# Second accumulator banks for the up products, bias columns inside evictions, and a gathered modulation in a diffusion step

## The chip, the cores and the metric

One core of a Trainium2 chip runs one step of a small hybrid diffusion network. The metric is the device time of one execution in microseconds.

## The reference

The input is 128 prompt and 512 latent tokens of 1024 features. Two layers each compute half a SwiGLU, a token mixer, and another half a SwiGLU. Before every sub-layer the tokens are normalised, scaled and shifted; scale, shift and gate (nine vectors of 1024 per layer, for two conditions) come from a linear map of the condition:

```python
def ada_modulation(cond, w, b):
    m = jax.nn.silu(cond) @ w + b
    return m.reshape(cond.shape[0], 1, 9, D_MODEL)

def half_ffn(x, g, mod, j, w13, w2):
    gt, up = jnp.split(ada_norm(x, g, mod, j) @ w13, 2, axis=-1)
    return x + 0.5 * mod[:, :, 3 * j + 2] * ((jax.nn.silu(gt) * up) @ w2)
```

Layer 0 mixes by windowed attention and a long convolution side by side, layer 1 by a gated DeltaNet in both directions. All is float32.

## The kernel before, in words

Everything is feature-major: a tile is 128 features by 640 tokens, and a product of 640 tokens is made in two halves of 320 in two banks of PSUM. Each float32 operand is split into a rounded part (hi) and a rest (lo), and a product is hi x hi, hi x lo and lo x hi. The weights are split on the chip: line 452 (ScalarE) makes hi and line 453 (VectorE) makes lo. The split weights lie in a ring of six slots.

A feed-forward part (`ffn_s`, four of them) handles the 22 feature tiles of the hidden layer in chunks of 7, 7 and 8. For each tile the gate and the up projection are one 2 x 2 block product, done with seven products of half the depth in place of eight, in the order q0, q3, q4, q1, q5, q2, q6. Each q is 12 matmuls of 322 columns (320 tokens and two columns that carry the shift's product, the bias, for the two conditions). q0 and q1 go to bank a, q3 and q2 to c, q4 to d, q5 to e, and q6 to d again; these are banks 4 to 7 for every tile but the second:

```python
a, c, d, e = [self.ps[:, b, :] for b in ((2, 3, 0, 1) if ci == 0 and m == 1 else range(4, 8))]
dst = (a, a, c, c, d, e, d)[q]
```

ScalarE copies q0 and q3 out of PSUM (line 783). VectorE evicts q4 (789), q1 (798), q5 (793), q2 (802) and q6 (807) over 320 columns, and the bias columns by a small operation of their own after each (791, 800, 794, 808). GpSimd adds and scales (795, 796, and 809 after 807). Line 803 scales on VectorE, and lines 804 and 805 are Silu on ScalarE. `finish` multiplies (756, 757, of which 756 reads what 809 writes) and splits (758, 759). It is called when q3 of the next tile has been written. The sums of weights that the seven products need are four GpSimd operations a tile (447); they read the loaded weights and the sums' buffers are read by lines 452 and 453.

After a chunk's up products its down products follow: eight feature tiles t, each of 42 or 48 matmuls (line 482) into a pair of banks that `wide` hands out in turn, 0 and 1 or 2 and 3. `x_add` (737) adds each to the residual in three operations: prompt, latent tokens of the first half, second half.

The first part also makes most of layer 0's modulation vectors. `ada_small` is a generator that `ffn_s` advances by one step before each q. A block is 128 features: two loads of 256 KB (577, on SP's queue, which also issues the weights' loads at 463), eight small matmuls (582), an eviction (584), a transpose (587), and on VectorE a reduction (551) and a bias (552). There are 48 blocks of three steps, with banks 0 and 1 in turn.

Each engine works its instructions off in a fixed order, which a scheduler makes at build time from the program's order and a priority; line 453's split, for one, is moved ahead by 30 and line 783 by 150.

## Time and profile before

| what | value |
|---|---|
| runs | 3068.59, 3074.09, 3074.75 us, median 3074.09 |
| profiled execution, its span | 3072.3 us, 1.8 below the median |
| TensorE, VectorE busy | 94%, 74% |
| ScalarE, GpSimd busy | 42%, 38% |

The profiled execution is one execution; the page gives no time of its own for it beside the span. The page has the busy shares first, then the groups by line with the idle time before them and what ended it. A time view shows instructions in order with their start in microseconds from the span's start. PE is TensorE, PEld its weight loads, DVE VectorE, ACT ScalarE, POOL GpSimd, SPq the queue of loads that SyncE issues.

### The profile page before, as it was taken

Reading aid. Unit: us, or ns where it says so; the run is one execution under the profiler, and the core shown is the slowest. Engines: PE = TensorE matmul, PEld = TensorE weight load, DVE = VectorE, ACT = ScalarE, POOL = GpSimd, SP = SyncE. Lnnn points to the kernel's source line nnn. Section 1 sums busy time; section 2 is a strip of 40 time slices with the busy share of each in tenths; the row PEclk is TensorE's granted clock in tenths of the full one; section 3 lists DMA queues with packets and bytes.
Section 4 is the critical chain, followed back from the end, with each engine's and each line's share of the span. In section 5 each row is a group of like instructions: output and inputs, shape, how many; then the busy total and the mean of one; then the engine's idle time right before and its main releaser. Section 6 shows DMA issues by size and latency. Waiting matters only on the chain. (4 is left out here: it accounts for less than half of the span.)

```text
span 3072.3 us, 54018 instructions
## 1 busy us (share of the span) xinstructions
PE 2903.3 (94%) x20612; PEld 2683.4 (87%) x20612; DVE 2263.2 (74%) x5235; ACT 1303.0 (42%) x2678; POOL 1158.2 (38%) x955
## 2 busy tenths in 40 slices
PE   5999999999989899999999999999998999999999
PEld 3999999977766899999899999978878888899999
DVE  6858586687865785858785858679898967858584
ACT  4424243466522342424342424445555544424241
POOL 3525253101222563535563535332222224626361
PEclk7999999999989999999999999999999999999999
DMA  5434353334375122222122222322211112222222
GB/s 202 141 107 150 105 158 121 122 105 125 100 274 206 63 72 84 85 74 89 50 74 85 84 75 84 131 91 70 72 59 34 34 37 94 68 77 74 84 70 83
DMA packets 109439, 300.80 MB, mean 98 GB/s; under 512 B 11803, under 2 KB 31963, under 8 KB 104444
## 3 DMA queue, kind: packets, MB, share of 16 engines
q1 hardware_dynamic: 109180, 297.35, 29.1%
q8 instruction: 162, 2.65, 0.4%
q14 instruction: 97, 0.79, 0.1%
HBM read 277.38 MB, written 19.93 MB: 97 GB/s over the span
## 5 line engine op out<-in xcount | busy, mean ns | idle before, releaser
L453 DVE TENSOR_TENSOR wh<-base,wh 128x512 fp32r<-128x512 f32 (+2 forms) x746 | 745.7, 1002 | 122.0 <-PE psum L482 62.6
L452 ACT ACTIVATE wh<-base 128x512 fp32r<-128x512 f32 (+2 forms) x779 | 533.7, 706 | 669.1 <-PE psum L482 400.8
L447 POOL TENSOR_TENSOR base<-base 128x512 f32<-128x512 f32 x352 | 518.1, 1476 | 683.9 <-DMA base<-w 364.1
L482 PE MATMUL psum<-G,wh 128*128 128x320 f32 x4992 | 742.5, 310 | 8.5 <-DVE base L737 8.0
L482 PEld LDWEIGHTS psum<-G,wh 128*128 128x128 f32 x4992 | 737.0, 188 | 13.4 <-issue 7.5
L778 PE MATMUL psum<-H,wh 128*128 128x322 f32 x4224 | 700.7, 317 | 22.6 <-ACT H L659 11.8
L778 PEld LDWEIGHTS psum<-H,wh 128*128 128x128 f32 x4224 | 648.0, 192 | 41.6 <-ACT H L659 13.8
L778 PE MATMUL psum<-HX,wh 128*128 128x322 f32 x3168 | 527.5, 316 | 27.5 <-DVE base L808 21.7
L778 PEld LDWEIGHTS psum<-HX,wh 128*128 128x128 f32 x3168 | 482.0, 191 | 44.0 <-issue 31.8
L482 PE MATMUL psum<-H,wh 128*128 128x322 f32 (+1 forms) x2448 | 476.7, 330 | 3.6 <-DVE base L722 2.1
L482 PEld LDWEIGHTS psum<-H,wh 128*128 128x128 f32 x2448 | 375.3, 193 | 25.8 <-issue 17.7
L737 DVE SCALAR_TENSOR_TENSOR base<-psum,base 128x128 f32<-128x128 f32 x336 | 127.1, 433 | 211.6 <-PE psum L482 211.5
L453 POOL TENSOR_TENSOR wh<-base,wh 128x1024 fp32r<-128x1024 f32 x33 | 82.2, 2491 | 239.5 <-ACT wh L452 234.8
L795 POOL TENSOR_TENSOR base<-base 128x320 f32<-128x320 f32 x88 | 113.1, 1285 | 143.4 <-DVE base L794 133.6
L805 ACT ACTIVATE base<-base 128x512 f32<-128x512 f32 x88 | 63.6, 723 | 204.0 <-DVE base L803 204.0
L758 ACT ACTIVATE G<-base 128x640 fp32r<-128x640 f32 x88 | 65.1, 740 | 167.0 <-DVE base L757 156.8
L756 DVE SCALAR_TENSOR_TENSOR base<-base 128x128 f32<-128x128 f32 x88 | 32.9, 374 | 120.0 <-POOL base L809 120.0
L694 POOL TENSOR_TENSOR base<-base 128x640 f32<-128x640 f32 x30 | 77.7, 2589 | 110.9 <-ACT base L692 94.7
L796 POOL TENSOR_TENSOR base<-base 128x320 f32<-128x320 f32 x88 | 87.8, 998 | 6.9
L809 POOL TENSOR_TENSOR base<-base 128x320 f32<-128x320 f32 x88 | 76.2, 866 | 28.9 <-DVE base L808 28.9
L803 DVE TENSOR_TENSOR base<-base 128x320 f32<-128x320 f32 x88 | 85.1, 967 | 0.4
L759 DVE TENSOR_TENSOR G<-base,G 128x640 fp32r<-128x640 f32 x88 | 71.8, 816 | 15.0 <-ACT G L758 14.9
(702 smaller groups left out, 3764.6 us busy)
## 6 DMA issues: line engine op xcount, KB each, us to landing
base<-w SPq DMA_DIRECT2D x208, 512.0 KB, 3.2
base<-ada_w SPq DMA_DIRECT2D x128, 256.0 KB, 3.7
base<-w SPq DMA_DIRECT2D x64, 448.0 KB, 3.3
base<-dn_in SPq DMA_DIRECT2D x33, 512.0 KB, 3.3
base<-ada_w SPq DMA_DIRECT2D x14, 1024.0 KB, 5.0
G<-ada_w SPq DMA_DIRECT2D x48, 256.0 KB, 3.5
HX<-ada_w SPq DMA_DIRECT2D x10, 1024.0 KB, 4.9
base<-mx_in SPq DMA_DIRECT2D x18, 512.0 KB, 3.3
```

Of the source, the lines that this page charges most:

```text
L447: nc.gpsimd.tensor_tensor(out=out, in0=x, in1=y, op=op)
L452: nc.scalar.activation(out=hi, in_=src, func=AF.Copy)
L453: (self.lo_eng if q is None else nc.vector).tensor_tensor(out=lo, in0=src, in1=hif, op=ALU.subtract)
L482: nc.tensor.matmul(ps[:, h, :n], lhsT=w[:, k, :], rhs=m[k][:, HALF * h:HALF * h + n], start=start and k == 0 and w is hi and m is mh, stop ...
L694: nc.gpsimd.tensor_tensor(out=self.acc.f, in0=self.acc.f, in1=sq, op=ALU.add)
L737: nc.vector.scalar_tensor_tensor(out=xt[:, xo:xo + n], in0=ps[:, h, o:o + n], scalar=gate[:, t, c:c + 1], in1=xt[:, xo:xo + n], op0=ALU.mu ...
L759: TT(out=gl[m], in0=tu, in1=gf[m], op=ALU.subtract)
L778: nc.tensor.matmul(dst[:, :HB], lhsT=w[:, i, :], rhs=v[:, i, :], start=not more and i == 0 and n == 0, stop=i == 3 and n == 2, skip_group_ ...
L795: nc.gpsimd.tensor_tensor(out=p5, in0=u2[:, 0, :HALF], in1=p5, op=ALU.add)
L796: nc.gpsimd.tensor_tensor(out=u2[:, 1, :HALF], in0=p5, in1=fac[:, 1], op=ALU.mult)
L803: TT(out=g2[:, 1, :HALF], in0=g2[:, 1, :HALF], in1=fac[:, 1], op=ALU.mult)
L809: nc.gpsimd.tensor_tensor(out=u2[:, 0, :HALF], in0=u2[:, 0, :HALF], in1=fac[:, 0], op=ALU.mult)
```

## The change

- The up products: bank pairs (4, 5) and (2, 3) alternate from tile to tile for a and c; d is 6, e is 7, and q6 has bank 0 to itself.
- The bias columns are evicted with their 320 columns, by one operation of 322; the buffers are longer by the two columns, and the scale is 1.0 in them. Silu and the product in `finish` take the bias from there. Silu is three operations in place of two, since the two bias columns lie in the middle.
- The two halves of a wide product lie side by side over the border of two banks (192 to 512 of the first, 0 to 320 of the second), so `x_add` takes two operations.
- `ada_four` replaces `ada_small` in the first part: four blocks gather in one bank, then one eviction, four transposes, one reduction and one bias for the four. Its next loads are issued after a block's matmuls. 48 blocks take two steps each, three where the four are full. It has bank 1, and the wide products of this part have banks 2 to 5.

```diff
         self.modA = [arena.alloc(48) for _ in range(2)]
-        self.rstd, self.rms = [arena.alloc(NT) for _ in range(2)]
+        self.rstd, self.rms = [arena.alloc(2 * HB) for _ in range(2)]
+        nc.gpsimd.memset(self.rms.f[:, HALF:HB], 1.0)
...
         self.mm_i += 1
-        return self.ps[:, b:b + 2, :]
+        return self.ps[:, b:b + 2, :].rearrange("p b n -> p (b n)")[:, 512 - HALF:]
...
                         n = HALF + extra * h
-                        nc.tensor.matmul(ps[:, h, :n], lhsT=w[:, k, :], rhs=m[k][:, HALF * h:HALF * h + n],
+                        nc.tensor.matmul(ps[:, HALF * h:HALF * h + n], lhsT=w[:, k, :], rhs=m[k][:, HALF * h:HALF * h + n],
...
 
-    def ada_bufs(self, A, low=False):
-        return [A.alloc(n, low) for n in (512, 512, 128)]
+    def ada_four(self, items, rg, bufs):
+        nc = self.nc
+        e = bufs[2].f
+        sc = self.scond.f.rearrange("p (k m) -> p k m", m=32)
+        todo = [(l, 2 * j + q, b) for l, j in items for q in range(2) for b in range(4)]
+        def load(i):
+            l, n, b = todo[i]
+            for h in range(2):
+                nc.sync.dma_start(out=bufs[h].f, in_=self.io["ada_w"][l, n, h][:, 512 * b:512 * b + 512])
+        load(0)
+        yield 0.0
+        for i, (l, n, b) in enumerate(todo):
+            p = rg.bank()
+            for h in range(2):
+                for g in range(4):
+                    nc.tensor.matmul(p[32 * g:32 * g + 32, 128 * b:128 * b + 128], lhsT=sc[:, 4 * h + g, :], rhs=bufs[h].f[:, 128 * g:128 * g + 128],
+                                     start=h == 0, stop=h == 1, tile_position=(0, 32 * g))
+            if i + 1 < len(todo):
+                load(i + 1)
+            yield 450.0
+            if b == 3:
+                nc.scalar.activation(out=e, in_=p, func=AF.Copy)
+                yield 0.0
+                self.ada_turn(l, n, e, rg)
+                yield 440.0
+            else:
+                yield 0.0
+        for b in bufs:
+            b.free()
+    def ada_bufs(self, A, low=False, n=128):
+        return [A.alloc(n, low) for n in (512, 512, n)]
...
         if self.sums is None:
-            self.sums, self.fac = [self.A.arenas[0].alloc(n, True) for n in (2048, NT)]
+            self.sums, self.fac = [self.A.arenas[0].alloc(n, True) for n in (2048, 2 * HB)]
+            self.nc.gpsimd.memset(self.fac.f[:, HALF:HB], 1.0)
...
         nc = self.nc
-        for (h, o, n, xo, c) in ((0, 0, NP, 0, 0), (0, NP, HALF - NP, NP, 1), (1, 0, HALF, HALF, 1)):
-            nc.vector.scalar_tensor_tensor(out=xt[:, xo:xo + n], in0=ps[:, h, o:o + n], scalar=gate[:, t, c:c + 1],
-                                           in1=xt[:, xo:xo + n], op0=ALU.mult, op1=ALU.add)
+        for c, v in enumerate((slice(0, NP), slice(NP, NT))):
+            nc.vector.scalar_tensor_tensor(out=xt[:, v], in0=ps[:, v], scalar=gate[:, t, c:c + 1], in1=xt[:, v], op0=ALU.mult, op1=ALU.add)
...
         part = [A.alloc(n, True) for n in (HB, HALF)]
-        tmp = [[A.alloc(NT, True) for _ in range(2)] for _ in range(2)]
+        tmp = [[A.alloc(2 * HB, True) for _ in range(2)] for _ in range(2)]
...
 
-        def finish(m, tg, tu, bu):
-            nc.vector.scalar_tensor_tensor(out=tu[:, :NP], in0=tu[:, :NP], scalar=bu[:, 0:1], in1=tg[:, :NP], op0=ALU.add, op1=ALU.mult)
-            nc.vector.scalar_tensor_tensor(out=tu[:, NP:], in0=tu[:, NP:], scalar=bu[:, 1:2], in1=tg[:, NP:], op0=ALU.add, op1=ALU.mult)
-            nc.scalar.activation(out=gh[m], in_=tu, func=AF.Copy)
-            TT(out=gl[m], in0=tu, in1=gf[m], op=ALU.subtract)
+        def finish(m, tg, tu):
+            for k, v in enumerate((slice(0, NP), slice(NP, NX))):
+                nc.vector.scalar_tensor_tensor(out=tg[:, v], in0=tu[:, v], scalar=tu[:, HALF + k:HALF + k + 1], in1=tg[:, v],
+                                               op0=ALU.add, op1=ALU.mult)
+            v = halves(tg)[:, :, :HALF]
+            nc.scalar.activation(out=halves(gh[m]), in_=v, func=AF.Copy)
+            TT(out=halves(gl[m]), in0=v, in1=halves(gf[m]), op=ALU.subtract)
...
                 p1, p5, tg, tu = [b.f for b in part + tmp[ti % 2]]
+                g2, u2 = halves(tg), halves(tu)
+                first = ci == 0 and m == 0
+                a, c = [self.ps[:, b, :] for b in ((4, 5), (2, 3))[ti % 2]]
+                d, e, d2 = [self.ps[:, b, :] for b in ((1, 7, 0) if ti == 1 and not ready else (6, 7, 0))]
                 ti += 1
-                g2, u2 = halves(tg), halves(tu)
-                a, c, d, e = [self.ps[:, b, :] for b in ((2, 3, 0, 1) if ci == 0 and m == 1 else range(4, 8))]
-                first = ci == 0 and m == 0
...
                     mh, ml, _ = P[q]
-                    dst = (a, a, c, c, d, e, d)[q]
+                    dst = (a, a, c, c, d, e, d2)[q]
...
                             fac = halves(self.norm.f)
-                        TT(out=g2[:, 1, :HALF], in0=d[:, :HALF], in1=p1[:, :HALF], op=ALU.add)
-                        bu = self.bias2()
-                        TT(out=bu, in0=d[:, HALF:HB], in1=p1[:, HALF:], op=ALU.add)
+                        TT(out=g2[:, 1], in0=d[:, :HB], in1=p1, op=ALU.add)
                     elif q == 5:
-                        TT(out=u2[:, 0, :HALF], in0=e[:, :HALF], in1=g2[:, 1, :HALF], op=ALU.add)
-                        TT(out=bu, in0=e[:, HALF:HB], in1=bu, op=ALU.add)
+                        TT(out=u2[:, 0], in0=e[:, :HB], in1=g2[:, 1], op=ALU.add)
                         nc.gpsimd.tensor_tensor(out=p5, in0=u2[:, 0, :HALF], in1=p5, op=ALU.add)
-                        nc.gpsimd.tensor_tensor(out=u2[:, 1, :HALF], in0=p5, in1=fac[:, 1], op=ALU.mult)
+                        nc.gpsimd.tensor_tensor(out=u2[:, 1, :HALF], in0=p5, in1=fac[:, 1, :HALF], op=ALU.mult)
                     if q == 1 and not first or q == 5 and first:
-                        TT(out=g2[:, 0, :HALF], in0=a[:, :HALF], in1=fac[:, 0], op=ALU.mult)
-                        bg = self.bias2()
-                        nc.vector.tensor_copy(out=bg, in_=a[:, HALF:HB])
+                        TT(out=g2[:, 0], in0=a[:, :HB], in1=fac[:, 0], op=ALU.mult)
...
                         TT(out=g2[:, 1, :HALF], in0=c[:, :HALF], in1=g2[:, 1, :HALF], op=ALU.add)
-                        TT(out=g2[:, 1, :HALF], in0=g2[:, 1, :HALF], in1=fac[:, 1], op=ALU.mult)
-                        nc.scalar.activation(out=tg[:, :NP], in_=tg[:, :NP], func=AF.Silu, bias=bg[:, 0:1])
-                        nc.scalar.activation(out=tg[:, NP:], in_=tg[:, NP:], func=AF.Silu, bias=bg[:, 1:2])
+                        TT(out=g2[:, 1, :HALF], in0=g2[:, 1, :HALF], in1=fac[:, 1, :HALF], op=ALU.mult)
+                        for v, k in ((slice(0, NP), 0), (slice(NP, HALF), 1), (slice(HB, NX), 1)):
+                            nc.scalar.activation(out=tg[:, v], in_=tg[:, v], func=AF.Silu, bias=tg[:, HALF + k:HALF + k + 1])
                     if q == 6:
-                        TT(out=u2[:, 0, :HALF], in0=d[:, :HALF], in1=u2[:, 0, :HALF], op=ALU.add)
-                        TT(out=bu, in0=d[:, HALF:HB], in1=bu, op=ALU.add)
-                        nc.gpsimd.tensor_tensor(out=u2[:, 0, :HALF], in0=u2[:, 0, :HALF], in1=fac[:, 0], op=ALU.mult)
-                        tail = (m, tg, tu, bu)
+                        TT(out=u2[:, 0], in0=dst[:, :HB], in1=u2[:, 0], op=ALU.add)
+                        nc.gpsimd.tensor_tensor(out=u2[:, 0, :HALF], in0=u2[:, 0, :HALF], in1=fac[:, 0, :HALF], op=ALU.mult)
+                        tail = (m, tg, tu)
...
 
+        s.wides = [2, 4]
...
         g = s.ffn_s(0, 0, lambda t, xt, tn, sq: s.make_h(t, 0, 1, xt, tn, sq), True,
-                    s.ada_small([(0, j) for j in range(2, 8)], s.ring(0, 1), s.ada_bufs(arena, True)), ready)
+                    s.ada_four([(0, j) for j in range(2, 8)], s.ring(1), s.ada_bufs(arena, True, 512)), ready)
         run(g)
+        s.wides = [0, 2]
```

VectorE's order in the second part, from the end of one tile's evictions into the next tile. Before:

```order
L453 TENSOR_TENSOR wh<-base,wh 128x512
L803 TENSOR_TENSOR base<-base 128x320
L807 TENSOR_TENSOR base<-psum,base 128x320
L808 TENSOR_TENSOR base<-psum,base 128x2
L756 SCALAR_TENSOR_TENSOR base<-base 128x128
L453 TENSOR_TENSOR wh<-base,wh 128x512
L757 SCALAR_TENSOR_TENSOR base<-base 128x512
L453 TENSOR_TENSOR wh<-base,wh 128x512
```

Now (454 is 453 before, 835 is 803, 839 is 807, 791 is 756 and 757):

```order
L454 TENSOR_TENSOR wh<-base,wh 128x512
L835 TENSOR_TENSOR base<-base 128x320
L839 TENSOR_TENSOR base<-psum,base 128x322
L454 TENSOR_TENSOR wh<-base,wh 128x512
L791 SCALAR_TENSOR_TENSOR base<-base 128x128
L791 SCALAR_TENSOR_TENSOR base<-base 128x514
L454 TENSOR_TENSOR wh<-base,wh 128x512
```

A conversion of weights now stands between q6's eviction and the product in `finish`; the other conversions kept their places.

TensorE's order in the first part, up products with the blocks of modulation between them. Before:

```order
L582 MATMUL psum<-base 32x128 x8
L778 MATMUL psum<-H,wh 128x322 x12
L587 MATMUL psum<-base 128x128
L778 MATMUL psum<-HX,wh 128x322 x12
L778 MATMUL psum<-H,wh 128x322 x12
L582 MATMUL psum<-base 32x128 x8
```

Now (613 is 582 before, 815 is 778, 1153 is the transposes):

```order
L613 MATMUL psum<-base 32x128 x8
L815 MATMUL psum<-H,wh 128x322 x24
L1153 MATMUL psum<-base 128x128 x4
L815 MATMUL psum<-HX,wh 128x322 x12
L613 MATMUL psum<-base 32x128 x8
L815 MATMUL psum<-H,wh 128x322 x12
L815 MATMUL psum<-HX,wh 128x322 x12
L613 MATMUL psum<-base 32x128 x8
```

There were 36 up products between two blocks and a transpose with each; now there are 24, and 36 with four transposes after each fourth block. The transposes come 24 products after the fourth block and 12 before the next.

## Rows read from the trace of the kernel before

**Rows 1.** Page, costliest groups: line engine op, names, shapes xcount | busy, mean ns | idle before
```profile
L482 PE MATMUL psum<-G,wh 128*128 128x320 f32 x4992 | 742.5, 310 | 8.5 <-DVE base L737 8.0
```

**Rows 2.** Waits of TensorE, 1000 to 2000 us: us in total, times, longest
```profile
PE psum L778 <- DVE base L808: 12.6, 21, 0.8
```

**Rows 3.** Order of time, tile of part two: start us, us, instruction xcount [idle before]
```profile
1255.58 0.35 DVE L756 SCALAR_TENSOR_TENSOR base<-base 128x128 f32<-128x128 f32 x1 [2.14 <-POOL base L809]
...
1260.56 0.15 DVE L791 TENSOR_TENSOR base<-psum,base 128x2 f32<-128x2 f32 x1
1260.62 0.68 DVE L453 TENSOR_TENSOR wh<-base,wh 128x512 fp32r<-128x512 f32 x1
...
1262.40 2.99 POOL L447 TENSOR_TENSOR base<-base 128x512 f32<-128x512 f32 x2 [4.05 <-DVE wh L453]
...
1262.76 1.49 DVE L453 TENSOR_TENSOR wh<-base,wh 128x512 fp32r<-128x512 f32 x1
...
1267.59 1.29 POOL L447 TENSOR_TENSOR base<-base 128x512 f32<-128x512 f32 x1
1267.60 1.78 PEld L778 LDWEIGHTS psum<-HX,wh 128*128 128x128 f32 x12 [1.05 <-issue]
1267.63 2.02 PE L778 MATMUL psum<-HX,wh 128*128 128x322 f32 x12 [0.82 <-DVE base L808]
...
1268.84 0.75 POOL L809 TENSOR_TENSOR base<-base 128x320 f32<-128x320 f32 x1
...
1269.63 0.35 DVE L756 SCALAR_TENSOR_TENSOR base<-base 128x128 f32<-128x128 f32 x1 [2.14 <-POOL base L809]
```

**Rows 4.** Order of time, line 807: first and last of 24 long tiles
```profile
1140.17 0.48 DVE L807 TENSOR_TENSOR base<-psum,base 128x320 f32<-128x320 f32 x1
...
2988.86 0.48 DVE L807 TENSOR_TENSOR base<-psum,base 128x320 f32<-128x320 f32 x1
```

**Rows 5.** Order of time, part one: modulation blocks, their loads (SPq), transposes, reduction
```profile
240.57 0.14 PEld L587 LDWEIGHTS psum<-base 128*128 128x128 f32 x1
...
243.17 0.16 DVE L551 TENSOR_REDUCE base<-psum 128x2 f32<-128x8 f32 x1
...
244.49 0.64 PE L582 MATMUL psum<-base 128*32 128x128 f32 x16
...
245.30 0.33 SPq L463 DMA_DIRECT2D base<-w  x1
245.72 0.86 SPq L577 DMA_DIRECT2D base<-ada_w  x2
...
264.11 0.65 PE L582 MATMUL psum<-base 128*32 128x128 f32 x16
...
264.59 0.80 SPq L577 DMA_DIRECT2D base<-ada_w  x2
...
270.33 0.64 PE L582 MATMUL psum<-base 128*32 128x128 f32 x16
```

**Rows 6.** Line 577: landing of the second load at 265.0, first load at 245.7
```profile
DMA to landing us min/median/max: 3.4/3.4/3.4
...
DMA to landing us min/median/max: 4.2/4.2/4.2
```

**Rows 7.** Waits of TensorE's weight loads, 66 to 489 us
```profile
PEld psum L587 <- ACT base L584: 4.5, 8, 0.9
```

**Rows 8.** Order of time, part two, end of a chunk's up and down products
```profile
1303.20 5.91 PEld L482 LDWEIGHTS psum<-G,wh 128*128 128x128 f32 x40
...
1304.02 0.15 DVE L808 TENSOR_TENSOR base<-psum,base 128x2 f32<-128x2 f32 x1
...
1352.48 3.61 PEld L778 LDWEIGHTS psum<-H,wh 128*128 128x128 f32 x24
...
1353.81 1.13 DVE L737 SCALAR_TENSOR_TENSOR base<-psum,base 128x128 f32<-128x128 f32 x3
```

**Rows 9.** Page, costliest groups: the residual adds
```profile
L737 DVE SCALAR_TENSOR_TENSOR base<-psum,base 128x128 f32<-128x128 f32 x336 | 127.1, 433 | 211.6 <-PE psum L482 211.5
```

16 lines of the change are left out of this document (8 added, 8 removed).

## The prediction, before the result was known

> **What bounds the kernel now.** I read the page's busy shares first, then the groups by line, then TensorE's waits, and last the order of time around one tile. TensorE is busy nearly all the time, so the change can only win what TensorE loses in waits, and can lose whatever new waits it makes. The down products are almost free of waits: 4992 of them waited 8.5 us in all, 8.0 of it for the residual add at line 737 [rows 1]. The up products wait mostly for line 808, the last two bias columns of bank d: 12.6 us, 21 times, in the second and third feed-forward part together [rows 2].
>
> The steady tile shows what stands behind that wait [rows 3]. The reader is to see two loops there. One is TensorE's: q6's eviction runs late on VectorE, and the next product into its bank d waits for line 808 until 1267.63; its weight load had stood idle for 1.05 us. The other has no TensorE in it. VectorE stands idle for 2.14 us at line 756 until GpSimd's line 809 is done; 809 is the last of a row that GpSimd works through from 1262.40 without a gap (two sums of weights, 795, 796, one sum, 809) to 1269.59, 7.2 us. The row starts when VectorE's conversion before it is done, and from line 756 at 1255.58 VectorE needs 6.8 us to get there. 7.2 + 6.8 is the tile's period: 1255.58 to 1269.63, 14.05 us. TensorE alone would need 7 x 1.78 (the weight loads of 12 products [rows 3]) = 12.5 us. In the second to fourth part 24 tiles took 13.9 us or more, the first and last of them ending at line 807 in [rows 4], and nine 13.1 to 13.5. The first part differs: there the modulation's products are added to TensorE's, and one block of them follows the other every 6.22 us, from 264.11 to 270.33 [rows 5].
>
> **The change part by part**, against the profiled span of 3072.3 us, which lies 1.8 us below the median of the runs (3074.09; I add these 1.8 at the end).
>
> *Banks of the up products.* The waits for lines 802 and 808 go. But what is late next is the VectorE and GpSimd loop, and no bank is part of it. The reordered row shows what it gains: of the small operations, 791 and 800 lie in its VectorE half and cost 0.06 us each there (1260.56 to 1260.62 [rows 3]; the listed 0.15 overlaps its successor), so 0.13; and one conversion, 0.60 us, moves from behind the wait to ahead of it. That gives 14.05 - 0.73 = 13.3 us, if the moved conversion doesn't delay GpSimd. It may: beside GpSimd a conversion took 1.49 us in place of 0.68, and GpSimd's two sums took 2.99 us, where one alone takes 1.29 [rows 3]; so two contended conversions cost GpSimd 0.4 us, 0.2 each. The lower bound of the delay is 0, the upper the whole conversion, 0.6. I take 0.35, between the 0.2 seen and the 0.6: a period of 13.65, 0.4 less. 24 x 0.4 + 9 x 0.2 = **-11 us**, bounds -4 (delay 0.6) and -28 (0, and all 33 tiles); -60 if TensorE's own 12.5 us became the pace, which the loop excludes.
>
> The Trainium skill, SBUF — State Buffer, section Who interferes with whom, says that a VectorE operation with two SBUF inputs and a GpSimd operation that reads SBUF lock each other out for a whole instruction. The trace partly agrees: 1262.76 + 1.49 is what a conversion of 0.6 takes that waits for the first of the two sums; the sums themselves lost less than it asks. By that rule the delay is 0.6, and this term -4.
>
> *Banks shared with the down products.* Before, the up products of a later tile sat in banks 4 to 7 and the down products in 0 to 3. Now q6 has bank 0. In parts two and three the first down product of each chunk goes to bank 0 and must wait for q6's eviction: its weight load started at 1303.20, line 808 ended at 1304.17 [rows 8]; 0.9 x 6 = 5 us. And once in each of parts one to three the next chunk's first tile takes the two banks of the last down product, whose residual add ran from 1353.81 to 1354.94 while the tile's products had started at 1352.48 [rows 8]; three conversions stand ahead of that add now, so 2.5 to 3 us: 9. What follows is a stretch that the loop above bounds, which absorbs part; I take half of 14, **+7**, bounds +3 and +14.
>
> *Modulation gathered.* The same 48 blocks of 8 products and as many transposes. The block's own price is in the spacing: 6.22 us less 12 products (1.78) and a transpose (0.14 [rows 5]) leaves 4.3 us between blocks that now have 24 products between them; 36 of the 47 gaps are so. A block needs the loads that may only start when the block before has read its buffers. Here SP's queue decides: the first load was issued 0.48 us after the block's start (264.11, 264.59), the second 0.4 later, landing 3.4 us after that [rows 5, 6]: 4.4 us for the half that is needed at 4.5. So undisturbed it fits with nothing to spare. Disturbed it doesn't: at 244.49 a weight load stood ahead in SP's queue (245.30), the first modulation load left at 245.72 and took 4.2 us, the second half a microsecond later: 5.9 us, 1.4 late [rows 5, 6]. Weight loads come twice a tile, blocks three times. Bounds 0 and 1.4 for each of 36; with three in ten disturbed like that row it is 0.4, which I take, nearer to the undisturbed row: **+14 us**, bounds 0 and +50.
>
> The four transposes write the bank that the next block's products take 12 products later. VectorE's reduction started 2.6 us after its transpose (240.57, 243.17 [rows 5]); three more transposes and 12 products are 2.2 us, so 0.5 us x 12, **+6**, bounds 0 and +12. TensorE waited 4.5 us for the small evictions ahead of transposes [rows 7]; these come once in four blocks now, **-4**. The 36 dropped evictions, reductions and bias adds free ScalarE and VectorE, which the first part hides. The blocks run out after 109 steps in place of 144, so the last 5.6 tiles of the part have none and run at the loop's 13.65 instead of TensorE's 12.5, the first of them from weights made ahead: **+4**, bounds 0 and +7.
>
> *Residual adds.* 336 adds of 433 ns [rows 9] become 224 over the same columns. What one instruction costs beyond its columns is at least the 0.06 us above and at most the 433 ns; I take 0.2 us, 112 times. In the down stretches VectorE waits for TensorE (211.5 us before these adds [rows 9]), so this is hidden; what shows is where TensorE waits for line 737 (8.0 us [rows 1]) and the last tile of a part: **-3**, bounds -6 and 0. The third Silu piece lengthens ScalarE's work, of which no step stands in the loop; the memsets come twice in the kernel, and two more columns in an eviction are counted at nothing, since the two that stand in the loop are there instead of the small operations.
>
> Sum: -11 + 7 + 14 + 6 - 4 + 4 - 3 = +13, so 3085.3 in the profile, 3087 as a median.
>
> **The rivals.** (1) *The banks were the limit and the loads fit.* If SP's order lets the loads go at once (0.1 us a block, +4; reductions +2) and the loop takes the moved conversion free (-24), with +4 for shared banks, +4 - 4 and -5 for the adds: -19, 3055. It decides at a block spacing of 4.5 us and a tile of 13.2. For it: the undisturbed load does fit. Against it: the rows at 244.49. 0.30. (2) *Cancel.* Loads at half my price (+6), reductions +2, the rest as taken: +1, 3075, within 0.2% (6 us, about what can be told from no change). 0.22. (3) *The lock.* The moved conversion holds GpSimd up for all its 0.6 us, the wait at the finish only changes its place, and the up tiles stay at 13.9: the term falls from -11 to -4, 3094. For it: the conversion's 1.49 us. Against it: the sums' small loss. 0.16. The Trainium skill's rule above is this rival. That the banks change nothing at all, since the loop and not TensorE sets the tile, is the end of this rival.
>
> **How the numbers follow.** Forecast 0.32, rivals 0.30, 0.22, 0.16. Slower by over 0.2%: 0.32 + 0.16 = 0.48; same 0.22; faster 0.30. The forecast's own range is 3080 to 3100. The range reaches from 3050, a little below rival 1, to 3110, where the loads cost 1.0 us a block.
>
> **What would show it.** In the changed profile: no wait of an up product for an eviction of d or c; the finish still waiting for GpSimd's product with the scale, by about 1 us after a conversion; tiles of 13.5 to 13.8 us. Modulation blocks 4.3 us apart where undisturbed, and TensorE waiting for their loads 10 to 20 us in all: none of that, and the forecast falls to rival 1. First down products waiting 0.9 us for the eviction of q6. If the tiles run at 12.5 us, my reading of the loop is wrong.

## The result, and the profile after it

The changed kernel takes 3100.24 us (median of 4 runs, 3097.39 to 3100.99) against 3074.42 for the kernel before on the same chip (4 runs, 3068.59 to 3075.91). The ratio is 1.0078, 95% interval 1.006 to 1.0096: slower, by 26 us. The profiled execution has a span of 3097.9 us, 2.3 below that median, against 3072.3.

First the two spans cut at the first matmul of each part's up products and at the end of the up products of parts one and three. The rows are, in order: part one, the stretch to part two (with the last down products and the first mixer), part two, part three, the second mixer, part four to the end. Columns: the stretch and its length, then busy time and instructions of PE, PEld, DVE, ACT and POOL, the granted clock, the DMA share and GB/s. The kernel before:

```profile
63.60:488.20 424.60, 420.04 (x3320) 398.01 (x3321) 304.80 (x612) 172.91 (x324) 181.90 (x148) 0.99 0.42 131
488.20:1056.40 568.20, 542.94 (x3585) 444.50 (x3584) 394.80 (x1036) 248.96 (x497) 136.23 (x175) 0.98 0.42 143
1056.40:1516.10 459.70, 443.94 (x2914) 434.57 (x2914) 340.28 (x604) 183.33 (x328) 228.96 (x176) 0.99 0.23 76
1516.10:1919.60 403.50, 388.37 (x2530) 380.11 (x2530) 301.57 (x528) 161.85 (x292) 195.58 (x155) 0.98 0.24 78
1919.60:2603.60 684.00, 633.32 (x5231) 577.62 (x5230) 557.79 (x1825) 340.57 (x891) 189.12 (x120) 0.98 0.21 69
2603.60:3072.30 468.70, 446.93 (x2913) 436.72 (x2912) 319.52 (x559) 168.13 (x297) 200.78 (x154) 0.99 0.23 76
```

The changed kernel:

```profile
63.50:507.80 444.30, 424.80 (x3321) 397.60 (x3322) 285.00 (x437) 171.28 (x311) 179.91 (x148) 0.99 0.40 125
507.80:1073.50 565.70, 544.61 (x3584) 445.37 (x3583) 398.03 (x1021) 247.68 (x494) 137.93 (x179) 0.98 0.43 143
1073.50:1536.70 463.20, 443.32 (x2914) 436.01 (x2913) 340.84 (x494) 186.20 (x349) 229.16 (x176) 0.99 0.23 76
1536.70:1947.90 411.20, 389.02 (x2531) 381.33 (x2530) 303.79 (x422) 165.89 (x315) 196.41 (x155) 0.98 0.23 76
1947.90:2633.60 685.70, 633.36 (x5231) 578.68 (x5230) 550.50 (x1813) 339.38 (x890) 190.65 (x121) 0.98 0.21 69
2633.60:3097.90 464.30, 442.01 (x2913) 434.76 (x2912) 316.26 (x443) 171.41 (x319) 195.65 (x154) 0.99 0.23 77
```

Read the lengths: part one +19.7, part two +3.5, part three +7.7, part four -4.4, the two mixers -2.5 and +1.7. So 20 of the 26 us lie in part one; the first mixer and part four win 7 us, and the rest of the loss lies mostly in part three. VectorE has 106 to 175 instructions fewer in each feed-forward part, but its busy time is the same in parts two and three (340.28 and 340.84, 301.57 and 303.79): what the small operations cost has come back in other rows. The clock is the same.

TensorE's waits in parts two and three (who waited for what, then us in total, times and the longest, as in [rows 2]):

```profile
PE psum L815 <- ACT base L820: 32.8, 25, 3.7
...
PE psum L483 <- DVE base L839: 2.0, 4, 0.5
...
PE psum L483 <- DVE base L772: 0.6, 1, 0.6
```

Line 820, ScalarE's copies of the q0 and q3 products (line 783 before), has taken the place of line 808 [rows 2]. Line 839 is q6's eviction, which the first down product of a chunk now waits for; line 772 is the residual add, as line 737 in [rows 1]. In part one there are new rows: one for the gathered blocks' loads, one for their reduction, and one for the residual add of the two banks that a tile shares with the last down product:

```profile
PE psum L613 <- DMA base<-ada_w: 15.2, 21, 2.5
...
PE psum L613 <- DVE base L552: 0.8, 1, 0.8
PE psum L815 <- DVE base L772: 0.7, 1, 0.7
```

The steady tile of part two, in order of time, to be set beside [rows 3]:

```profile
1254.45 0.48 DVE L834 TENSOR_TENSOR base<-psum,base 128x320 f32<-128x320 f32 x1
...
1256.15 1.17 DVE L835 TENSOR_TENSOR base<-base 128x320 f32<-128x320 f32 x1
1257.24 0.48 DVE L839 TENSOR_TENSOR base<-psum,base 128x322 f32<-128x322 f32 x1
1258.47 1.40 DVE L454 TENSOR_TENSOR wh<-base,wh 128x512 fp32r<-128x512 f32 x1 [0.75 <-ACT wh L453]
1260.52 2.03 DVE L791 SCALAR_TENSOR_TENSOR base<-base 128x128 f32<-128x128 f32 x2 [0.65 <-POOL base L840]
...
1268.48 0.48 DVE L834 TENSOR_TENSOR base<-psum,base 128x320 f32<-128x320 f32 x1
```

```profile
1252.61 3.07 POOL L448 TENSOR_TENSOR base<-base 128x512 f32<-128x512 f32 x2 [4.89 <-DMA base<-w]
...
1257.04 1.03 POOL L830 TENSOR_TENSOR base<-base 128x320 f32<-128x320 f32 x1
1258.02 1.30 POOL L448 TENSOR_TENSOR base<-base 128x512 f32<-128x512 f32 x1
1259.29 1.20 POOL L840 TENSOR_TENSOR base<-base 128x320 f32<-128x320 f32 x1
1260.45 1.29 POOL L448 TENSOR_TENSOR base<-base 128x512 f32<-128x512 f32 x1
1266.48 3.22 POOL L448 TENSOR_TENSOR base<-base 128x512 f32<-128x512 f32 x2 [4.75 <-DMA base<-w]
```

```profile
1262.64 0.74 ACT L794 ACTIVATE G<-base 128x640 fp32r<-128x640 f32 x1 [3.35 <-DVE base L791]
...
1263.81 0.41 ACT L820 ACTIVATE base<-psum 128x320 f32<-128x320 f32 x1
...
1264.28 2.05 PE L815 MATMUL psum<-H,wh 128*128 128x322 f32 x12 [0.41 <-ACT base L820]
```

The tile takes 14.03 us (line 834 from 1254.45 to 1268.48), as before. The loop of [rows 3] is still there with its two halves. GpSimd's row runs without a gap of note from 1252.61 to 1260.49, the end of line 840: 7.9 us where it was 7.2 [rows 3]. VectorE's half, from line 791 at 1260.52 to GpSimd's next row at 1266.48, is 6.0 us where it was 6.8.

Over half of these 6.0 us is not VectorE's work but a load. The load of the next weights leaves SP's queue when the conversion behind the finish has read their buffer (line 454, done at 1263.15). It lands 3.2 us later, and GpSimd's row starts 0.1 us after that:

```profile
1262.47 0.68 DVE L454 TENSOR_TENSOR wh<-base,wh 128x512 fp32r<-128x512 f32 x1
...
1263.17 0.33 SPq L464 DMA_DIRECT2D base<-w  x1
...
DMA to landing us min/median/max: 3.2/3.2/3.2
```

It was so in the kernel before. There the load left at 1258.92 and landed 3.3 us later, 0.1 us before the row at 1262.40. [rows 3] names the conversion that ended at 1262.37 as the releaser, but one tile earlier the same row started while that conversion was still running:

```profile
1247.78 0.68 DVE L453 TENSOR_TENSOR wh<-base,wh 128x512 fp32r<-128x512 f32 x1
...
1248.33 3.00 POOL L447 TENSOR_TENSOR base<-base 128x512 f32<-128x512 f32 x2 [3.90 <-DMA base<-w]
...
1258.92 0.33 SPq L463 DMA_DIRECT2D base<-w  x1
```

Line 840 took 1.20 us beside the conversion that now stands ahead of the finish; its counterpart took 0.75 [rows 3]. TensorE's wait hangs on the same loop: line 820's second copy stands in ScalarE's queue behind line 794, which waits for line 791.

TensorE doesn't meet this tile at once. The first tiles of a chunk run at its own 12.55 us, from weights made ahead, and the 14 us set in when these are used up. In the changed kernel that is sooner: from first matmul to first matmul, the third to fifth tile of part three's second chunk took 13.98, 14.05 and 14.02 us, where they had taken 12.55, 13.10 and 14.03.

### The profile page after: what moved, and what is told of

It is laid out like the page before. It is cut to its first block, busy times and chain, and to the rows that moved or that the text cites. A ratio compares the mean times of both kernels' runs of the same rounds, so it can differ in the third digit from the quotient of the medians.

```text
span 3097.9 us, 53236 instructions
## 1 busy us (share of the span) xinstructions
PE 2904.3 (94%) x20612; PEld 2685.4 (87%) x20612; DVE 2238.9 (72%) x4699; ACT 1308.8 (42%) x2728; POOL 1155.1 (37%) x958
## 3 DMA queue, kind: packets, MB, share of 16 engines
q8 instruction: 162, 2.65, 0.4%
## 5 line engine op out<-in xcount | busy, mean ns | idle before, releaser
L454 DVE TENSOR_TENSOR wh<-base,wh 128x512 fp32r<-128x512 f32 (+2 forms) x746 | 711.9, 956 | 195.3 <-ACT wh L453 79.4
L453 ACT ACTIVATE wh<-base 128x512 fp32r<-128x512 f32 (+2 forms) x779 | 528.6, 703 | 675.1 <-PE psum L483 423.2
L448 POOL TENSOR_TENSOR base<-base 128x512 f32<-128x512 f32 x352 | 495.7, 1412 | 684.7 <-DMA base<-w 417.2
L772 DVE SCALAR_TENSOR_TENSOR base<-psum,base 128x128 f32<-128x128 f32 x224 | 113.2, 547 | 222.5 <-PE psum L483 222.5
L837 ACT ACTIVATE base<-base 128x128 f32<-128x128 f32 (+2 forms) x264 | 115.9, 470 | 274.1 <-DVE base L835 200.9
L791 DVE SCALAR_TENSOR_TENSOR base<-base 128x128 f32<-128x128 f32 (+1 forms) x176 | 148.3, 882 | 48.7 <-POOL base L840 48.7
L829 POOL TENSOR_TENSOR base<-base 128x320 f32<-128x320 f32 x88 | 109.6, 1245 | 163.3 <-DVE base L828 151.3
L840 POOL TENSOR_TENSOR base<-base 128x320 f32<-128x320 f32 x88 | 97.0, 1102 | 43.8 <-DVE base L839 43.8
L830 POOL TENSOR_TENSOR base<-base 128x320 f32<-128x320 f32 x88 | 87.6, 996 | 6.9
```

Of the source, the lines that this page charges most:

```text
L448: nc.gpsimd.tensor_tensor(out=out, in0=x, in1=y, op=op)
L453: nc.scalar.activation(out=hi, in_=src, func=AF.Copy)
L454: (self.lo_eng if q is None else nc.vector).tensor_tensor(out=lo, in0=src, in1=hif, op=ALU.subtract)
L772: nc.vector.scalar_tensor_tensor(out=xt[:, v], in0=ps[:, v], scalar=gate[:, t, c:c + 1], in1=xt[:, v], op0=ALU.mult, op1=ALU.add)
L791: nc.vector.scalar_tensor_tensor(out=tg[:, v], in0=tu[:, v], scalar=tu[:, HALF + k:HALF + k + 1], in1=tg[:, v], op0=ALU.add, op1=ALU.mult)
L829: nc.gpsimd.tensor_tensor(out=p5, in0=u2[:, 0, :HALF], in1=p5, op=ALU.add)
```

## The experiments

Twelve kernels, in three groups of four. All ratios are to the kernel before, run on the same chip in the same group; it took 3074.4 to 3075.1 us in the three groups, so medians of different groups are set side by side. Lengths are from one profile each, part one and parts two to four cut as above, but parts one and three only to the start of their last up product's last matmul (0.2 us less). A long tile is the time from one q6 eviction on VectorE to the next, where the weights made ahead are used up. Stretches that no edit touches give the spread of such a length: the second mixer took 678.0 to 691.4 us in the runs below, part two 463.2 to 466.2 in three kernels that are the same there (changed, small blocks, blocks three apart). So a part's difference below 3 us is not read as an effect.

| kernel | median us | ratio, 95% interval | part one | two | three | four | long tile |
|---|---|---|---|---|---|---|---|
| before | 3074.4 | | 424.4 | 459.7 | 403.4 | 468.8 | 13.9 to 14.3 |
| changed | 3100.2 | 1.0078 (1.006 to 1.0096) | 444.2 | 463.2 | 411.1 | 464.3 | 14.0 |
| small blocks | 3084.3 | 1.0035 (1.0017 to 1.0053) | 423.2 | 466.2 | 408.9 | 466.2 | 14.0 |
| blocks three apart | 3082.7 | 1.0025 (1.0007 to 1.0043) | 426.9 | 466.1 | 408.6 | 464.8 | 14.0 |
| pairs turned round | 3093.7 | 1.005 (1.0029 to 1.007) | 442.1 | 464.5 | 408.1 | 467.5 | 14.0 |
| no alternation | 3102.0 | 1.0091 (1.0069 to 1.0112) | 443.4 | 461.8 | 406.5 | 464.6 | 14.0 |
| no alternation, small blocks | 3080.3 | 1.0027 (1.0009 to 1.0046) | 424.4 | 460.6 | 406.1 | 466.0 | 14.0 |
| finish later in the text | 3093.3 | 1.0059 (1.0041 to 1.0078) | 443.9 | 465.1 | 406.8 | 463.2 | 14.0 |
| finish held back | 3051.0 | 0.9925 (0.9903 to 0.9947) | 435.0 | 452.6 | 396.8 | 451.4 | 13.24 |
| held back, no alternation | 3060.5 | 0.9947 (0.9927 to 0.9966) | 441.4 | 449.8 | 396.1 | 454.6 | 13.24 |
| before, finish later in the text | 3072.8 | 0.9986 (0.9971 to 1.0001) | 425.4 | 459.3 | 403.0 | 465.5 | 13.9 to 14.3 |
| before, held back | 3077.9 | 1.0011 (0.9993 to 1.0029) | 422.6 | 462.6 | 405.7 | 469.8 | 14.17 to 14.4 |
| no sums | 3028.3, one run | | 436.8 | 443.2 | 384.8 | 446.8 | 12.55 |
| three edits together | 3036.9 | 0.9892 (0.9876 to 0.9907) | 421.1 | 451.8 | 393.2 | 452.4 | 13.24 |

**Part one: is it the loads?** The modulation put back into small blocks:

```diff
-                    s.ada_four([(0, j) for j in range(2, 8)], s.ring(1), s.ada_bufs(arena, True, 512)), ready)
+                    s.ada_small([(0, j) for j in range(2, 8)], s.ring(1), s.ada_bufs(arena, True)), ready)
```

> The changed kernel with the modulation of part one made as before, in small blocks with an eviction, a transpose and a reduction each, in bank 1. Theory A (the gathered blocks cost time because each waits for loads that may only start when the block before has read its buffers): TensorE's wait for the modulation's loads in part one (15.2 us, and 23.8 us at the weight loads, in the changed kernel) goes to below 3 us, part one ends at 488 to 494 us in place of 508.0, and the kernel takes 3081 to 3088 in place of 3100. Rival B (part one is longer for its up products: banks shared with the down products, ScalarE's queue): part one still ends at 503 or later, and the kernel stays at 3095 to 3102.

Measured: 16 us less than the changed kernel; part one 423.2, as before the change, and no wait for the modulation's loads in its list. The other parts stay as they were. That is theory A, but it takes the gathering away together with its load waits. So a second kernel keeps the gathering and only gives the loads more time:

```diff
                 yield 440.0
             else:
+                yield 0.0
                 yield 0.0
```

> The changed kernel with the gathered blocks three steps apart in place of two (36 products between the loads of one block and the next in place of 24, 144 steps in place of 109); nothing else. Theory A (the blocks wait for loads that are issued one block ahead): the wait of line 613 for its loads falls from 15.2 us to below 2, part one (428 us from its first to its last tile) takes 408 to 414, the kernel 3080 to 3088, as with the small blocks. Rival B (gathering itself costs: three transposes and three blocks of products write a bank that the reduction and the eviction hold): part one stays at 420 or more, 3092 to 3102.

Measured: 18 us less, part one 426.9. TensorE's waits at line 613:

```profile
PE psum L613 <- DVE base L552: 3.9, 6, 1.7
PE psum L613 <- DMA base<-ada_w: 1.3, 3, 0.6
```

The load wait falls from 15.2 to 1.3, and part one by 17.3 us, 13.9 of it in this wait: so much do loads cost that may leave only one short block ahead. Gathering as such costs little: part one is 3.7 us longer than with small blocks, and the reduction's wait is 3.9 here. (This edit also spreads the blocks over the whole part, as the small ones are.)

**The shared banks.** The pairs turned round:

```diff
-        s.wides = [2, 4]
+        s.wides = [4, 2]
...
+        s.wides = [2, 0]
         run(s.ffn_s(0, 1, lambda t, xt, tn, sq: s.make_s(t, 1, 0, xt, tn, sq), False))
...
+        s.wides = [0, 2]
         s.rg = s.ring(4, 5, 6, 7)
         run(s.mixer1(lambda t, xt, tn, sq: s.make_s(t, 1, 2, xt, tn, sq)))
```

> The changed kernel with the order of the two bank pairs of the down products turned round in parts one to three, so that in parts two and three the first down product of a chunk goes to banks 2 and 3 and the last to 0 and 1, as it already is in part four. Theory A (shared banks cost the 6 and 8 us that parts two and three lost, where part four, which starts in banks 2 and 3, won 1.9): parts two and three are 4 to 6 us shorter each, 3088 to 3093; first up products wait no more for line 772, first down products no more for line 839. Rival B (what the shared banks cost is taken in by the loop behind them, and parts two and three lose elsewhere): less than 2 us a part, 3096 to 3102.

Measured: the wait of down products for line 839 (2.0 us in four places) is gone from the list, but parts two and three are 1.3 longer and 3.0 shorter, no more than the spread; of the 6 us by which the median is lower, 4.4 lie in the second mixer of the profile, which the edit doesn't touch. Neither theory's range is met. No up product waits for line 772 in these parts. Then the whole alternation taken away:

```diff
-                a, c = [self.ps[:, b, :] for b in ((4, 5), (2, 3))[ti % 2]]
-                d, e, d2 = [self.ps[:, b, :] for b in ((1, 7, 0) if ti == 1 and not ready else (6, 7, 0))]
+                a, c = [self.ps[:, b, :] for b in ((2, 3) if ti == 1 else (4, 5))]
+                d, e, d2 = [self.ps[:, b, :] for b in ((1, 7, 0) if ti == 1 and not ready else (6, 7, 0 if ti == 1 else 6))]
```

> The changed kernel without the alternation: all tiles but the second take banks 4 and 5, and q6 goes to bank 6 as q4 does; the evictions with bias columns, the two residual adds and the gathered modulation stay. Theory A (the loop sets the tile and no bank is part of it): tiles stay at 14.0, TensorE waits for line 839 or 820 by some 0.5 to 1 us a tile, and what the banks shared with the down products cost (1.6 to 2.3 us a part by the run with the pairs turned round) is gone: 3090 to 3100. Rival B (the alternation hides something that the loop does not show): tiles of 14.3 us or more, 3105 to 3120.

Measured: 3102.0, no different from the changed kernel, tiles at 14.0. Parts two and three are 6.0 us shorter together and the second mixer is 5.6 longer in this profile; the median lies just above theory A's range. Rival B's 14.3 us a tile is out. TensorE's wait for q6's eviction comes back as the row below, 0.2 us at a time, and costs nothing, since TensorE waits for line 820 in the same tiles anyway:

```profile
PE psum L815 <- DVE base L839: 3.6, 20, 0.2
```

Without alternation and with small blocks, what is left are the evictions with their bias columns, the third Silu piece and the two residual adds (both edits above together):

> The changed kernel without the alternation of banks and with the modulation in small blocks as before: what is left of the change are the bias columns in the evictions, the third Silu piece and the two residual adds. Theory A (the loop of VectorE and GpSimd gives back what the small operations and the residual adds save): within 0.3% of the kernel before, 3072 to 3083, tiles at 14.0 us. Rival B (these edits carry a gain that the other two parts of the change hide): 3050 to 3066.

Measured: 3080.3, tiles at 14.0: theory A. These edits by themselves win nothing either; the kernel is still 6 us slower than the one before (interval 1.0009 to 1.0046), and no single part shows why. Every part of the change sits at the same 14.0 us.

**What holds the tile at 14.0?** The finish, moved to a later place in the program text:

```diff
-                    if tail and (q == 3 or m == nf - 1 and q == 6):
+                    if tail and (q == 1 or m == nf - 1 and q == 6):
```

> The changed kernel with one step put off: the finish of a tile (its two multiplications, the copy and the difference) comes after the fourth product of the next tile and no longer after the second. Theory A (the tile's 14.0 us are a loop of VectorE and GpSimd: VectorE stops at the finish until GpSimd's product with the scale is done, and GpSimd's next row waits for the conversions queued behind the finish): VectorE's wait ahead of line 791 (48.7 us) falls to below 5, TensorE's wait for the copies of line 820 (32.8 us in part two and three) with it, long tiles go from 14.0 to 12.5 to 13.0 us, 33 tiles win 1.0 to 1.4 us each: 3050 to 3070. Rival B (ScalarE is what holds TensorE: line 820's copies stand in its queue behind the Silu pieces): the tile stays at 13.8 to 14.0, TensorE goes on waiting for line 820 and the kernel takes 3092 to 3102.

Measured: 14.0 us, but this doesn't separate the theories: VectorE's order was the same in all but a few tiles. I take it that the scheduler had placed the finish by its own estimate of when VectorE is free; no run shows that. The steady tile still has line 791 in its old place, with 0.65 us of waiting for line 840. In the one tile of parts two to four where the order did change, the second, it fell from 13.5 to 12.26 us. The same edit in the kernel before changed as little:

> The kernel before with the same step put off (finish after the fourth product of the next tile). Theory A (the loop of VectorE and GpSimd, and not the banks, sets the tile of the kernel before as well): VectorE's 120.0 us of waiting ahead of line 756 mostly go, TensorE's waits for line 808 too, long tiles fall from 13.9 to 14.2 to 12.5 to 13.0: 3025 to 3050. Rival B (the wait for line 808 is the bank's: q6 evicted late on VectorE for other reasons than the finish): TensorE goes on waiting for line 808 and the time stays at 3065 to 3078.

Measured: 3072.8, no change that can be told, tiles at 13.9 to 14.3. A data dependence was needed. The bias columns of the finished tile are rewritten by an operation that reads the next tile's bank, times zero:

```diff
-                    if tail and (q == 3 or m == nf - 1 and q == 6):
+                    if tail and (q == 4 or m == nf - 1 and q == 6):
+                        if q == 4:
+                            b = tail[2][:, HALF:HB]
+                            nc.vector.scalar_tensor_tensor(out=b, in0=dst[:, :2], scalar=0.0, in1=b, op0=ALU.mult, op1=ALU.add)
                         finish(*tail)
```

> The changed kernel with the finish of a tile held back until the third product of the next tile has been evicted: the two bias columns that it adds are first rewritten by a small VectorE operation that reads that product's bank, so that nothing can order it earlier. (Moving its place in the program text alone had left VectorE's order as it was in nearly all long tiles, 14.0 us each.) Theory A (the loop of VectorE and GpSimd sets the tile): VectorE's wait ahead of line 791 and TensorE's wait for line 820 go, long tiles fall from 14.0 to 12.5 to 13.2 us, 33 tiles win 0.8 to 1.5 us: 3050 to 3075. Rival B (GpSimd's own row and the conversions that it contends with are the pace, the place of the finish is of no matter): 13.8 to 14.1 us, 3093 to 3103.

Measured: 3051.0, 49 us below the changed kernel, inside theory A's range. Of these, 38 lie in parts two to four and 9 in part one. Long tiles are 13.24 us, just above the 12.5 to 13.2 expected. VectorE and GpSimd in order of time, one tile of part two (line 845 is the added operation):

```profile
1246.71 3.56 DVE L454 TENSOR_TENSOR wh<-base,wh 128x512 fp32r<-128x512 f32 x3 [0.75 <-ACT wh L453]
1250.20 0.48 DVE L826 TENSOR_TENSOR base<-psum,base 128x322 f32<-128x322 f32 x1
1250.60 0.15 DVE L845 SCALAR_TENSOR_TENSOR base<-psum,base 128x2 f32<-128x2 f32 x1
...
1251.27 1.00 DVE L791 SCALAR_TENSOR_TENSOR base<-base 128x128 f32<-128x128 f32 x2
```

```profile
1246.67 0.75 POOL L840 TENSOR_TENSOR base<-base 128x320 f32<-128x320 f32 x1
1248.05 1.68 POOL L448 TENSOR_TENSOR base<-base 128x512 f32<-128x512 f32 x1 [0.63 <-DVE wh L454]
...
1251.99 1.43 POOL L448 TENSOR_TENSOR base<-base 128x512 f32<-128x512 f32 x1 [2.26 <-DMA base<-w]
```

Line 840 ends at 1247.42, and the finish comes over 3 us later: it doesn't wait for GpSimd here any more (5.2 us ahead of line 791 in the whole execution, where it was 48.7). The loop through the finish was what held the tile at 14.0. TensorE's gaps in the seven tiles of part two's second chunk fell from 3.68 to 0.80 us in sum. What sets the 13.24 that is left is not separated: VectorE has 0.75 us of idle time in the tile, and GpSimd's row still starts when a load has landed (the last line above). A longer ring of buffers for the loaded weights, which would take the load out of the loop, was not tried. And the kernel before, held back in the same way (its two bias columns are `tail[3]`)?

> The kernel before with its finish held back in the same way. Theory A (the same loop, not the bank of q6, set its tile of 13.9 to 14.2 us): long tiles of 12.5 to 13.2, TensorE's waits for line 808 below 3 us, VectorE's 120 us ahead of line 756 below 20: 3030 to 3055. Rival B (the bank is the limit once the loop is loosened): TensorE still waits for line 808, tiles of 13.5 and more, 3062 to 3078.

Measured: 3077.9, no change: rival B by its numbers, though TensorE waits less for line 808 than for line 800, the bias columns of q1, which VectorE reaches late. The wait at the finish is gone there too (3.4 us ahead of line 756, where it was 120.0), but the tile is 14.17 us:

```profile
1241.90 0.48 DVE L807 TENSOR_TENSOR base<-psum,base 128x320 f32<-128x320 f32 x1
...
1242.36 4.19 DVE L453 TENSOR_TENSOR wh<-base,wh 128x512 fp32r<-128x512 f32 x3
...
1250.84 1.77 DVE L759 TENSOR_TENSOR G<-base,G 128x640 fp32r<-128x640 f32 x1
...
1256.09 0.48 DVE L807 TENSOR_TENSOR base<-psum,base 128x320 f32<-128x320 f32 x1
```

```profile
PE psum L778 <- DVE base L800: 28.8, 24, 3.0
...
PE psum L778 <- DVE base L808: 7.7, 29, 0.3
```

VectorE has next to no idle time from one line 807 to the next, 14.19 us: its own work, drawn out where it runs beside GpSimd, is the limit. So the two halves of the story need each other: the change freed VectorE, but only a kernel without the loop can use it. Which half of the change is it, the alternation or the evictions? The held-back finish without the alternation:

> The changed kernel with the finish held back, and without the alternation of banks (all tiles but the second on banks 4 and 5, q6 in bank 6). It asks which part of the change let the held-back finish pay 49 us here, when the kernel before gained nothing from it. Theory A (the alternation: TensorE would otherwise wait for the evictions of the tile before): tiles of 13.7 us or more, TensorE waiting for line 839 by over 10 us in all, 3065 to 3085. Rival B (the bias columns that ride in the evictions: they take four small VectorE operations out of a tile in which VectorE has no gap left): tiles stay at 13.2 to 13.3, and with the shared banks gone 3045 to 3053.

Measured: tiles at 13.24 as with the alternation, and parts two to four as long (1300.5 us in sum against 1300.8): so it isn't the alternation, and rival B holds for the tiles. But the small operations are only a part of it. VectorE's row in the tile of the kernel before held back is 1.8 us longer than in the changed kernel held back; 0.55 of that are the small operations, and 0.97 is line 759, which starts behind a sum of GpSimd's there (1.70 us to the next start) where its counterpart, line 795, starts ahead of one and takes 0.73. Where an operation falls beside the sums comes with the order, and no run separates the order from the evictions. The median is 9 us higher than with the alternation and outside both ranges; 6.4 of it lie in part one (441.4 against 435.0), where TensorE waited 12.3 us for the modulation's loads in place of 8.8. Why it waited longer stays open. Last, GpSimd's sums of weights are left out, all but the first:

```diff
-                if q == 0:
+                if q == 0 and j == 0:
```

> The changed kernel without GpSimd's four sums of weights, except for the first pair of tiles; the products of the other pairs use whatever stands in the room of the sums, so the result is left wrong in that part. Theory A (VectorE's conversions and GpSimd's sums hold each other up, which is why a conversion moved ahead of the finish gave its time back): the conversions of 1.38 and 1.40 us in a long tile fall to 0.6 to 0.7, the two multiplications of line 791 from 2.03 us together to 1.1, tiles to 12.5 to 12.8 us and the kernel to 3040 to 3060. Rival B (these conversions are long for something else, PSUM or their waits): they stay above 1.0 us.

Measured, in one execution: 3028.3 us, below theory A's range, and tiles of 12.55 us, TensorE's own 7 products. The same VectorE operations as in the steady tile above:

```profile
1260.16 0.48 DVE L835 TENSOR_TENSOR base<-base 128x320 f32<-128x320 f32 x1
1260.57 0.48 DVE L839 TENSOR_TENSOR base<-psum,base 128x322 f32<-128x322 f32 x1
1261.80 0.69 DVE L454 TENSOR_TENSOR wh<-base,wh 128x512 fp32r<-128x512 f32 x1 [0.75 <-ACT wh L453]
1262.40 1.01 DVE L791 SCALAR_TENSOR_TENSOR base<-base 128x128 f32<-128x128 f32 x2
```

The conversion of 1.40 us takes 0.69, line 835 falls from 1.17 to 0.48, the two multiplications of line 791 from 2.03 to 1.01. Line 834, which reads one operand from PSUM, took 0.48 in the middle of two sums (1254.45, above), and line 839 takes 0.48 in both kernels. So the contention is shown for each operation. The 72 us are not its price alone: without the sums GpSimd's half of the loop shrinks as well, and the held-back finish wins 49 us with all sums kept.

**A version that beats both.** The finish held back, the blocks three apart and the pairs turned round, together:

> The changed kernel with the three edits that had shortened it one by one: the finish held back until the third product of the next tile is evicted, the gathered blocks three steps apart, the two bank pairs of the down products turned round in parts one to three. If their gains add (49 us, 18 us and 3 to 7 us against 3100): 3026 to 3034, over 1% below the kernel before. If the looser up tiles bring the modulation's loads or the shared banks back (a shorter tile gives the loads less time): part one stays at 415 us or more and the kernel at 3036 to 3048.

Measured: 3036.9 us (3036.59 to 3037.34), ratio 0.9892, interval 0.9876 to 0.9907: 63 us below the changed kernel and 38 below the one before. The gains don't quite add: the number and part one's 421.1 us are those of the second case, but its cause isn't, for no wait for the modulation's loads is left in part one. The two gains overlap there: the held-back finish alone had already brought that wait from 15.2 to 8.8 us, so the longer spacing had less left to win (435.0 to 421.1, where it won 17.3 in the changed kernel). And the bound of 415 was careless, since the blocks three apart had measured 426.9 by themselves.

## Why the prediction was right, and where it wasn't

The forecast of 3087 within 3050 to 3110, slower, held: 3100. It lies at the upper edge of the forecast's own 3080 to 3100, and the change is twice the one forecast. The sign was earned by the loads, whose mechanism was right. The size came out of errors in both directions: the largest, in the loop and in parts two and three, made the kernel slower than the sum, and the reduction made it faster. Point by point:

- **Modulation loads, +14.** Right in mechanism, a little small. TensorE waited 15.2 us for them, and giving them time took 17.3 from part one. The step that SP's queue and one block's lead leave nothing to spare was the decisive one; rival 1 needed the loads to fit, and they didn't. The queue is half of it: about 8 of the 15 us fell where both loads had left within 1 us of their block's start and then landed late (the second one after 305.89 left in time and took 5.4 us, where I had taken 3.4); in the rest the second load left later, as I had read it. (The 4.4 us of the undisturbed case is 4.3 by its rows, 264.99 + 3.4 - 264.11; that changes nothing.)
- **Loop of VectorE and GpSimd, -11.** This step failed. I took 0.35 us for the delay by the moved conversion, with 0.6 as the most. GpSimd's row grew by 0.7 us (7.2 to 7.9) and VectorE's half shrank by 0.86 (6.8 to 5.96; I had taken 0.73). The tile stayed at 14.0 and the term is about nothing: part four, whose tiles had been 14.1 to 14.3, won 4.4; parts two and three, at 13.9 to 14.1, won none. That is rival 3, and its price of 3094 was nearer than the forecast. The mechanism behind it is the one that the run without sums shows: a VectorE operation with both inputs in SBUF takes about twice as long beside GpSimd's work, and line 840 took 1.20 us beside a conversion where it takes 0.75 without one. The Trainium skill, SBUF — State Buffer, section Who interferes with whom, gives this as an exclusive lock for two-input operations and none for operations with at most one SBUF input. The trace agrees in both (1.40 to 0.69, and 0.48 either way). I had weighed the sums' small loss of 0.4 us against it; line 840 alone lost 0.45 more. The reading of what starts GpSimd's row was wrong as well: it is the landing of a load and not the conversion that ended last. So the small operations 791 and 800, which I counted with 0.13 us, were not in the loop; they ran while the load was under way (from 1258.92 to 1262.3). From the finish to the load's issue VectorE's half shrank by 0.69 us (3.34 to 2.65). And two bounds don't follow from their rows: for -28, 33 x 0.73 is 24; for -60, 24 x 1.55 + 9 x 0.8 is 44.
- **TensorE's waits.** I expected no wait for d or c and none in their place but the finish. A wait for line 820 took their place, 32.8 us in parts two and three: TensorE waits wherever the loop reaches it, and the loop now reaches it through ScalarE's queue. I had written that no step of ScalarE's stands in the loop, and hadn't looked at what stands behind line 794 there.
- **Shared banks, +7.** The first down products wait, but 0.5 us a time and 2.0 in four places, not 0.9 in six. The other wait, of a tile for the residual add, comes once in part one (0.7 us) and not in parts two and three, where I had 3 us each. By the stretch it is a little more: the four stretches of down products that wait take 50.2 us in place of 49.44, 3.1 in sum. Taking the alternation away shortened parts two and three by 6.0 us in sum. Two more pairs of kernels in the table differ by the alternation alone and agree in the sign: 8.4 us with small blocks, 3.5 with the finish held back. Each alone could be the spread of such lengths; part four, which starts in the other bank pair, gets no shorter by more than 0.2 in any of them. So by single profiles the alternation costs these two parts 3.5 to 8.4 us, against 5.7 of my term (half of 0.9 x 6 and of two times 3): about right in size, though the rows that I had named show only a part of it. The medians don't settle it (1.8 and 9.5 us more without the alternation, 4.0 less with small blocks), since part one and the mixers move too.
- **Reduction, +6.** Too high: 0.8 us, once. I put the lag of one row [rows 5] on each of the 12. With the blocks three apart it is 3.9 us in six places. **Small evictions, -4.** No wait for one is left. **Last tiles of part one, +4.** Of the five tiles without blocks at the end, two came near the loop's pace (13.50 and 14.03 us against 12.55), 2.4 us. The last chunk's up products as a whole took 114.9 us where they had taken 116.9, since many of the blocks' own products have moved to the chunks before; I hadn't set that off.
- **Residual adds, -3.** Not seen: the first stretch of down products takes 49.44 us in both kernels, and TensorE's wait for line 772 is 7.6 us after 8.0 [rows 1]. They are hidden, as I had written.

The sum was +13 and the result is +26. Of the 13 that are missing, 7 are the loop (-4 where I had -11), 3 the loads, 3 the residual adds, and 5 to 6 are in parts two and three, which lost 11.2 where the shared banks were to cost 5.7; the reduction takes 5 back. If the alternation costs 3.5 to 8.4 us, 3 to 8 of the 11.2 stay open. The 14-us tiles set in sooner also without the alternation (12.91, 14.03 and 13.99 us for the third to fifth tile in part three's second chunk, where the kernel before had 12.55, 13.10 and 14.03); why the weights made ahead last shorter no run shows. Part three alone differs by 2.5 us among the three kernels that are the same there.

That the tile is a loop without TensorE and without any bank was right, and the runs show it: no alternation, no change (3102.0); finish held back, 49 us. What I missed is the load in the loop, and that behind the loop stands VectorE's own full row, so that the kernel before gains nothing from breaking it.

## What to carry to other kernels

When two engines off the critical engine hand work to each other, measure the loop they form before freeing banks or dropping small operations, and follow it through the loads that it starts. Here a free bank or a shorter queue didn't pay until the loop was cut, and cutting the loop paid only where VectorE's row was short. Moving a line in the text may leave the scheduled order as it was: look at the order, and force it with a data dependence if need be. And when blocks are packed closer, recount the lead of their loads: here 24 products between blocks were too few and 36 enough, for the same bytes.

## What the runs showed of the hardware that I had not expected

The contention between VectorE and GpSimd is larger than the trace of before had let me think. A conversion of 128x512 takes 0.69 us by itself and 1.40 beside GpSimd's work, while evictions with one input in PSUM, five of VectorE's sixteen operations in a tile, stay at 0.48 to 0.49. Without GpSimd's sums, 4 of its 7 operations in a tile, the up tile falls from 14.0 to 12.55 us and the kernel by 72 us in one execution; the contention is one part of that and GpSimd's shorter row another.

A load can be a step of such a loop without TensorE ever waiting for it: 3.2 us of the 14.0 are the landing of the weights that GpSimd's sums read.
